# A two-layer DiT block on one Trainium2 core: a new order for the mixer's second half, half a product moved ahead of a norm in the latents, and other PSUM banks behind the attention

## The chip, the cores and the metric

The kernel runs on one core of one Trainium2 chip. The core has five engines that each work through an instruction queue of their own: TensorE (PE in the profile, matrix products; PEld is the loading of its stationary operand), VectorE (DVE), ScalarE (ACT), GpSimd (POOL) and SyncE (SP, which issues the DMA transfers here). They meet through semaphores. Products land in PSUM, eight banks of 128 partitions x 512 fp32 numbers; all other data of the core lie in SBUF.

The metric is the device time of one launch in microseconds (us); lower is better. The kernel before takes 1628.01 us, the median of three runs from 1627.53 to 1628.06.

## The reference, cut to what matters

Batch 1, 512 tokens of width 1024, a context of 256 tokens, fp32 throughout. Layer 0 mixes tokens with a Fourier half and a Hyena half, on tokens and context; layer 1 is multi-head latent attention (16 heads) from the tokens to tokens and context. Each layer ends in a feed-forward network with a convolution of three taps.

```python
for i in range(2):
    sh1, sc1, g1, sh2, sc2, g2 = split(silu(c) @ w_mod[i] + b_mod[i], 6)      # and the same for the context
    hx = rms_norm(x, norm1[i]) * (1 + sc1) + sh1
    if i == 0:
        proj = hx @ w_in                                    # 1024 -> 2048
        y_f = fft2(proj[:, :512] by groups of 128, axes=(tokens, features)).real
        x0, x1, v = split(dwconv3(proj[:, 512:]), 3)        # three times 512
        y_h = x0 * long_conv(v * x1, spectrum, hy_bias)     # irfft(rfft(u) * spectrum)
        yx = concat(y_f, y_h) @ w_out
    else:
        a = hx @ mla_w_in                                   # 256 query latents, 128 + 32 of keys and values
        yx = softmax(q k^T / sqrt(96)) v @ mla_w_o          # q, k, v from the latents, each rms-normed
    x = x + g1 * yx
    x = x + g2 * ((silu(dwconv3(gate)) * val) @ w_down)     # gate, val = split(modulated rms_norm(x) @ w_up, 2)
```

The Fourier transforms are products with tables of cosines and sines on TensorE, folded by symmetry, so that the mixer is a chain of products with elementwise work between them.

## The kernel before, in words

**Products.** Every matrix is kept as a high and a low part (`wh`, `wl` of a weight `wr`; `hh`, `hl` of an activation), and `mm3` adds three products: high by high (line 158), high weight by low activation (159), low weight by high activation (160). ScalarE writes the high part (`hi`, line 133), VectorE the low one (`lo`, line 138; in the mixer some lows go to GpSimd). Weights come in by `wraw` (line 146) from SyncE's queue into three buffers `wr`, and are split into three buffers each of `wh` and `wl`. TensorE gets 128 partitions a time.

**PSUM.** A pool holds tiles by tag: `mm` has three buffers of two banks, `ms` two buffers of one bank. Which banks a tag has follows from the order in which the tags are first used after a pool was opened. In the attention another pool (`psB`) is open; it is closed in `layer1`, where `psA` is opened again.

**Mixer's second half** (about 219 to 313 us of the span). The order of work on TensorE, VectorE, ScalarE and GpSimd is written out: `MIX_ORDER` is a list of short step names, each of which records its instructions when its turn comes; nothing reorders them afterwards. The DMA steps (R) stand in the same list. The names:

- `P6q`, `P7q`: projection of row block 6 or 7, two of the eight steps over the width (six products each, 512 and 260 columns wide) per name, into an `mm` tile. `CAm`, `CBm`, `CCm`: the convolution of block m, on ScalarE (line 863), then twice on VectorE (865, 867).
- `FM`: x1 times v on GpSimd (871, 872). `FD`: its sums and differences on VectorE (878, 879). `T3`: six transposes on TensorE (887). `UH`, `UL`: high and low part of the result, `uTh`, `uTl`.
- `SC0`, `SC1`, `SX0` to `SX3`: spectra of context (C) and tokens (X), products of `uTh`, `uTl` with the table `u`, into `mm`. For each: `DA`, `DB` on VectorE (918, 919, 921), which multiply by the filter's spectrum into `sx`; `QA`, `QB` on GpSimd (926); `YA`, `YB` the high part on ScalarE; `LA` the low part on VectorE, `LB` on GpSimd.
- `IC0` to `IC3`, `IX0` to `IX3`: inverse transforms into `ms`. Each is followed by `..E` on ScalarE, `..S` on VectorE (961, 962), `..M` on VectorE (967), `..H` on ScalarE and `..L` on VectorE, which give `yh` and `yl` of row blocks 4 to 7.
- `FHg`, `FLg`: high and low part of the Fourier half's group g. `FAg`, `GAg`: its first transform, tokens and context, into `mm`; `PH`, `PL` and `GH`, `GL` (1014) the high and low parts `pqh`, `pql`. `FBg`, `GBg`: the second transform; `FE`, `GE` on ScalarE, `FS`, `GS` on VectorE (1040 to 1042).
- `WH`, `WL`, `TH`, `TL`: high and low parts of weights and tables. `ZHg`, `ZLg`: those of row blocks 0 to 3. `OA`, `OB0` to `OB3`: the first column block of the output product, over row blocks 4 to 7, then 0 to 3.

While this runs, VectorE also has a few row sums of the modulation (`gemv_dve`, line 243), recorded between these steps.

**Latents** (in `attention`, lines 1343 to 1375). `qa(k)` adds step k of the query latents, for two row blocks m (three products of 512 columns each), into one `mm` tile. `take(KD)` and `f2(tp, 0)` end the sums of squares of the second half's norm: each has TensorE multiply the last squares by ones (line 280, `ms<-ones,nt`), after which VectorE finishes the sum (283, 285) and does a reciprocal root of twelve small instructions (167 to 176); `f2(tp, 1)` spreads the result with TensorE (298). The order is again the written one.

**Behind the attention** (`layer1`). The last output product leaves row blocks 0 and 1 in a PSUM tile `k` (`pre` in the code) of `psB`. The residual `xr` is loaded back (line 1723), VectorE adds the two row blocks to it (1725), then `psA` is opened and `res_proj` does row blocks 2 to 7 in two halves of 256 tokens (eight steps, 24 products per block and half; line 1143 takes the tile away), while the norm of the first half runs in its hook. Then the feed-forward network follows.

Of the kernel before, what the change touches and what calls it, by code (L numbers as in the profile page):

```python
# [72 lines left out]
KAx3 G3 KBx3 SDAx2 RG4 SQx2 G4 SDAx0 SPBx2 KAx2 SPBx0 SDBx2 SQx0 KBx2 SDBx0  # L73
"""
MIX_ORDER = """
P11 R6 R7 WH6 WL6 P60 CA11 P61 CB11 CC11 P62 FM Ru0 WH7 FD T3 P63 WHu0 UH CA6 WL7 UL WLu0 CB6 SC0 Ru1 CC6 DBc0 SC1 DAc1 QBc0 YBc0 LBc0 WHu1 Ri0 Rn1
P70 QAc1 YAc1 WLu1 P71 DAc0 P72 QAc0 P73 YAc0 WHi0 SX0 LAc1 DBc1 HP QBc1 Rs0 LAc0 WLi0 SX1 CA7 YBc1 THn1 LBc1 CB7 DBx0 IC0 QBx0 DAx0 TLn1 IC1 QAx0 FH0
Rc0 THc0 ICE0 THs0 YBx0 ICE1 YAx0 Rn0 CC7 ICS0 LBx0 IC2 FL0 ICS1 TLs0 Rc1 IC3 THn0 LAx0 GA0 DAx1 DBx1 QAx1 SX2 GH0 QBx1 FA0 GL0 TLc0 THc1 YAx1 YBx1
LBx1 LAx1 FH1 TLn0 TLc1 DAx2 DBx2 SX3 PH0 GB0 ICM0 FH2 QAx2 QBx2 PL0 YAx2 ICH0 YBx2 LAx2 FL1 DAx3 GE0 ICE2 LBx2 DBx3 ICL0 FL2 FB0 FA1 FE0 GS0 PH1 QAx3
Ri1 GA1 QBx3 FS0 ICM1 PL1 YBx3 ICH1 FA2 WHi1 ICL1 ICE3 FB1 ICS2 LBx3 WLi1 GH1 YAx3 PH2 GL1 GA2 LAx3 Ro0 FE1 IX1 PL2 GB1 ICS3 ICM2 IXE1 IX0 IXS1 FH3  # L80
FS1 ICH2 ICM3 GH2 ICH3 ICL2 IXM1 IXH1 IXE0 ICL3 IX2 GE1 IXS0 FB2 FL3 GS1 IXE2 IXM0 GL2 FA3 FE2 IXH0 IXS2 IX3 IXM2 IXH2 FS2 GA3 PH3 IXL1 IXL0 PL3 IXL2
IXE3 IXS3 GB2 WHo0 IXM3 IXH3 FB3 GH3 GE2 FE3 WLo0 GL3 GB3 GE3 ZH0 IXL3 GS2 FS3 GS3 OA ZL0 OB0 ZH1 ZL1 ZH2 ZH3 OB1 ZL2 ZL3 OB2 OB3
"""


class Builder:
# [1182 lines left out]
    def attention(self, x, hh, hl, steps, aw):  # L1269
# [72 lines left out]
        with self.tc.manual_schedule(engines={ENG.PE, ENG.DVE, ENG.Activation, ENG.Pool}):  # L1342

            pqa = self.mm()

            def qa(k):
                for m in range(2):
                    wh, wl = aw[f"qa{m}"]
                    w = slice(128 * k, 128 * k + 128)
                    self.mm3(pqa[:, 512 * m : 512 * m + 512], wh[:, w], wl[:, w], hh[k][:, 0:T], hl[k][:, 0:T], k == 0, k == KD - 1)  # L1350

            def down(ps, h, l, m, k, c0, n):
                w = slice(m * k, m * k + m)
                self.mm3(ps[:m, c0 : c0 + n], h[:, w], l[:, w], hh[k][:, c0 : c0 + n], hl[k][:, c0 : c0 + n], k == 0, k == KD - 1)

            qa(0)
            qa(1)
            qa(2)
            take(KD)
            qa(3)  # L1360
            f2(tp, 0)
            wph, wpl = self.t(pt, [P, 512], F32R, "whpe", 1), self.t(pt, [P, 512], F32R, "wlpe", 1)
            self.hi(wph, wp[:, :512])
# [350 lines left out]
    def layer1(self, x, hh, hl, steps, aw):  # L1714
        nc, I = self.nc, self.I
        oh, ol, xd, pre = self.attention(x, hh, hl, steps, aw)
        nt = self.pool("nt", bufs=5)
        hp = self.pool("h2p")
        self.xp = self.pool("xres")
        tp = lambda: self.t(nt, [P, 512], F32, "nt")  # L1720
        x = [self.t(self.xp, [P, T], F32, f"xr{d}") for d in range(KD)]
        for d in range(KD):
            nc.sync.dma_start(x[d], xd[d])
        for m in range(2):
            nc.vector.scalar_tensor_tensor(x[m], pre[:, 512 * m : 512 * m + 512], self.mod[1][:, 16 + m, 0:1], x[m], op0=ALU.mult, op1=ALU.add)
        self.close("psB")
        self.ps = self.pool("psA", space=PSUM)
        half = [[(0, 256)], [(256, 256)]]
        hh = [self.t(hp, [P, T], F32R, f"hh{d}") for d in range(KD)]
        hl = [self.t(hp, [P, T], F32R, f"hl{d}") for d in range(KD)]  # L1730
        hook, rest = self.norm_hook(*[self.norm(1, 1, x, hh, hl, c, 256, tp) for c in (0, 256)])
        self.res_proj(1, 2, oh, ol, KD, lambda m: I["w_o"][m], x, half, hook, ready=2)
        rest()
        self.close("pO")
        self.close("pa")
        self.dbg("xa1", x)
        self.ffn(1, x, hh, hl, T, [(0, T)], half, None)
        return x
# [204 lines left out]
```

## Time and profile before

| | |
|---|---|
| median of three runs | 1628.01 us (1627.53 to 1628.06) |
| the profiled execution | 1633.3 us, its span 1631.5 us |
| mean granted TensorE clock | 0.991 |
| TensorE busy | 1589.6 us, 97% of the span |
| VectorE busy | 1048.2 us, 64% |
| ScalarE busy | 620.1 us, 38% |
| GpSimd busy | 109.5 us, 7% |
| mixer's second half | about 219 to 313 us |
| latents' query products and second norm | about 942 to 963 us |
| residual product behind the attention | about 1213 to 1257 us |

A line of the timeline has the start in us, the duration, the engine, the line of the code, the operation with output and inputs, the sizes, and in brackets how long the engine stood idle before it and what ended the wait. Durations overlap a little with the next row's start, since matmuls and VectorE's instructions are pipelined; the rate is read from start to start. A group over a stretch (`--windows` answers) has the busy time of each engine, the number of its instructions, the granted clock of TensorE (1.00 is full speed, 0.50 half) and the share of DMA.

### The profile page before, as it was taken

What the parts mean: (1) busy time and instruction counts of PE and PEld (TensorE: products, weight loads), DVE (VectorE), ACT (ScalarE), POOL (GpSimd) and SP (SyncE); (2) the same over time, 40 slices, a digit from 0 to 9 for tenths busy, and PEclk for the clock granted to TensorE, in tenths of its full rate; (3) what the DMA queues carried; (4) which work ended last, traced back from release to release, by engine and by line L of the source; (5) the groups of instructions that cost most, each with busy time, mean ns of one, the idle gap of its engine ahead of it and who ended that gap; (6) DMA issues with size and microseconds to landing.
All of it is one profiled execution on the core that took longest, in us unless ns stands there. A gap on an engine that the chain in (4) does not pass through costs nothing.

```text
span 1631.5 us, 20800 instructions
## 1 busy us (share of the span) xinstructions
PE 1589.6 (97%) x8248; PEld 1300.2 (80%) x8248; DVE 1048.2 (64%) x1702; ACT 620.1 (38%) x883; POOL 109.5 (7%) x165
## 2 busy tenths in 40 slices
PE   7999998999999999999999999999989999999999
PEld 5687888888888888888888887566559888888887
DVE  5788869878786354643354577899977544344243
ACT  4451224424222212222133337898953432233131
POOL 0112134000000000000000001121210000000000
PEclk9999998999999999999999999999999999999999
DMA  9336412533443243432342210000033232222222
GB/s 344 108 117 211 170 36 72 194 117 106 166 155 129 66 141 129 159 125 71 108 147 99 95 55 16 13 11 13 0 129 116 78 103 102 80 104 98 83 91 90
DMA packets 54542, 173.35 MB, mean 106 GB/s; under 512 B 6188, under 2 KB 9454, under 8 KB 53422
## 3 DMA queue, kind: packets, MB, share of 16 engines
q1 hardware_dynamic: 54445, 172.03, 30.5%
q8 instruction: 65, 1.06, 0.3%
q14 instruction: 32, 0.25, 0.0%
HBM read 166.24 MB, written 5.77 MB: 105 GB/s over the span
## 4 chain that ended last, share of the span: by engine, by line
PE 81%; DVE 13%; DMA 2%; issue 2%; ACT 1%; POOL 1%; SPq 0%; POOLq 0%; ACTq 0%; DVEq 0%
PE mm L158 24%; PE mm L159 23%; PE mm L160 23%; PE pv L1613 2%; DVE junk L243 2%; DVE S L1589 1%; DVE wl L138 1%; PE s L1559 1%; DVE wr L1628 1%; DMA wr<-w_in 1%; PE k L158 1%; PE k L159 1%; PE k L160 1%; DMA wm<-wmod0a 1%; PE mm L616 1%
## 5 line engine op out<-in xcount | busy, mean ns | idle before, releaser
L158 PE MATMUL mm<-hh,wh 128*128 128x512 f32 (+2 forms) x1360 | 480.9, 356 | 1.8 <-ACT wh L133 0.9
L159 PE MATMUL mm<-hl,wh 128*128 128x512 f32 (+2 forms) x1360 | 478.6, 353 | 2.3 <-DVE hl L313 2.3
L160 PE MATMUL mm<-hh,wl 128*128 128x512 f32 (+2 forms) x1360 | 478.4, 352 | 1.6 <-DVE wl L138 1.6
L133 ACT ACTIVATE wh<-wr 128x1024 fp32r<-128x1024 f32 (+1 forms) x192 | 197.8, 1033 | 579.8 <-PE mm L159 544.6
L138 DVE TENSOR_TENSOR wl<-wr,wh 128x1024 fp32r<-128x1024 f32 (+2 forms) x192 | 231.2, 1207 | 234.9 <-ACT wh L133 228.3
L158 PEld LDWEIGHTS mm<-hh,wh 128*128 128x128 f32 x1360 | 256.6, 189 | 48.4 <-issue 7.6
L159 PEld LDWEIGHTS mm<-hl,wh 128*128 128x128 f32 x1360 | 257.1, 189 | 39.2 <-DVE hl L313 3.5
L160 PEld LDWEIGHTS mm<-hh,wl 128*128 128x128 f32 x1360 | 256.9, 189 | 37.5 <-DVE wl L138 2.2
L243 DVE SCALAR_TENSOR_TENSOR junk<-wr,sb 128x1024 bf16<-128x1024 f32 x128 | 156.2, 1220 | 41.2 <-DMA wr<-wmodT 40.7
L158 PE MATMUL mm<-ah,wh 128*128 128x512 f32 (+1 forms) x480 | 172.4, 359 | 0.0
L160 PE MATMUL mm<-ah,wl 128*128 128x512 f32 (+1 forms) x480 | 172.2, 359 | 0.0
L159 PE MATMUL mm<-al,wh 128*128 128x512 f32 (+1 forms) x480 | 171.9, 359 | 0.0
L1143 DVE SCALAR_TENSOR_TENSOR xr<-mm,mod,xr 128x512 f32<-128x512 f32 (+1 forms) x100 | 61.8, 632 | 160.6 <-PE mm L160 160.1
L159 PEld LDWEIGHTS mm<-al,wh 128*128 128x128 f32 x480 | 90.5, 189 | 14.2 <-DVE al L138 0.2
L158 PEld LDWEIGHTS mm<-ah,wh 128*128 128x128 f32 x480 | 90.4, 188 | 14.1 <-issue 0.3
L160 PEld LDWEIGHTS mm<-ah,wl 128*128 128x128 f32 x480 | 90.4, 188 | 14.2
L1613 PE MATMUL pv<-S,V 128*128 128x512 f32 x192 | 93.9, 598 | 2.5 <-ACT S L1592 2.5
L1175 ACT ACTIVATE fg<-fg 128x772 f32<-128x772 f32 (+1 forms) x44 | 32.6, 741 | 98.0 <-DVE fg L375 91.4
L1567 ACT ACTIVATE S<-s,rks 128x512 f32<-128x512 f32 x96 | 62.6, 685 | 12.4 <-PE pv L1613 8.5
L1613 PEld LDWEIGHTS pv<-S,V 128*128 128x128 f32 x192 | 34.5, 190 | 34.7 <-issue 29.3
L1589 DVE TENSOR_TENSOR S<-S,mx 128x1536 f32<-128x1536 f32 x32 | 55.4, 1750 | 2.3 <-POOL mx L1585 2.3
L1585 POOL PARTITION_ALL_REDUCE mx<-mx x16 | 44.9, 2806 | 161.6 <-DVE mx L1582 161.6
(337 smaller groups left out, 2273.2 us busy)
## 6 DMA issues: line engine op xcount, KB each, us to landing
wr<-w_up SPq DMA_DIRECT2D x88, 512.0 KB, 3.2
wr<-wmodT SPq DMA_DIRECT2D x80, 512.0 KB, 3.2
wr<-w_dn SPq DMA_DIRECT2D x32, 512.0 KB, 3.2
wm<-wmod0a SPq DMA_DIRECT2D x8, 1024.0 KB, 8.9
wr<-w_in SPq DMA_DIRECT2D x16, 512.0 KB, 4.2
wr<-w_out SPq DMA_DIRECT2D x13, 512.0 KB, 3.7
wr<-w_dn SPq DMA_DIRECT2D x17, 384.0 KB, 3.0
wr<-w_o SPq DMA_DIRECT2D x11, 512.0 KB, 3.2
```

Source lines behind the costliest of these rows:

```text
L133: self.nc.scalar.activation(dst, src, AF.Copy)
L138: (eng or self.nc.vector).tensor_tensor(dst, src, hi.bitcast(F32), op=ALU.subtract)
L158: mmul(out, wh, xh, start=start, stop=False)
L159: mmul(out, wh, xl, start=False, stop=False)
L160: mmul(out, wl, xh, start=False, stop=stop)
L243: nc.vector.scalar_tensor_tensor(junk, raw, 1.0, self.sb[:, j, :], op0=ALU.mult, op1=ALU.mult, accum_out=acc)
L1143: nc.vector.scalar_tensor_tensor(x[m][:, a2:b2], ps[:, a2:b2], mod[:, 8 * sec + m, c : c + 1], x[m][:, a2:b2], op0=ALU.mult, op1=ALU.add)
L1175: nc.scalar.activation(g[:, :n], g[:, :n], AF.Silu)
L1567: nc.scalar.activation(c.S[a][j // 3][:, j % 3, :], c.ps[a, j], AF.Copy, scale=c.r[:, g : g + 1])
L1585: nc.gpsimd.partition_all_reduce(c.m[a][:, 1, :], c.m[a][:, 0, :], P, bass.bass_isa.ReduceOp.max)
L1589: v.tensor_tensor(c.S[a][h], c.S[a][h], mb.to_broadcast([P, 3, T]), op=ALU.subtract)
L1613: nc.tensor.matmul(c.P[a], V[:, j, o : o + 128], c.S[a][j // 3][:, j % 3, :], start=j == 0, stop=j == 5)
```

## The change

It has three parts. No instruction of the computation is added or removed; the sizes are the same.

**1. `MIX_ORDER` is written anew.** The same steps stand in another order, on all engines. The first two lines of the list, of before and after:

```diff
 MIX_ORDER = """
-P11 R6 R7 WH6 WL6 P60 CA11 P61 CB11 CC11 P62 FM Ru0 WH7 FD T3 P63 WHu0 UH CA6 WL7 UL WLu0 CB6 SC0 Ru1 CC6 DBc0 SC1 DAc1 QBc0 YBc0 LBc0 WHu1 Ri0 Rn1
-P70 QAc1 YAc1 WLu1 P71 DAc0 P72 QAc0 P73 YAc0 WHi0 SX0 LAc1 DBc1 HP QBc1 Rs0 LAc0 WLi0 SX1 CA7 YBc1 THn1 LBc1 CB7 DBx0 IC0 QBx0 DAx0 TLn1 IC1 QAx0 FH0
...
+P11 R6 WH6 R7 WL6 CA11 CB11 CC11 P60 FM P61 Ru0 FD T3 P62 WH7 UH P63 WHu0 CA6 Ru1 UL WL7 WLu0 CB6 SC0 CC6 DAc0 SC1 P70 P71 QAc0 YAc0 DAc1 LAc0 P72
+DBc0 QAc1 QBc0 Ri0 YAc1 LAc1 WHu1 DBc1 WLu1 Rs0 P73 YBc0 WHi0 CA7 QBc1 SX0 HP WLi0 Rn0 YBc1 CB7 THn0 SX1 LBc0 LBc1 Rn1 DBx0 DAx0 IC0 THs0 THn1 QBx0
...
```

TensorE had the products of block 6 with `T3` between P62 and P63; in the new list `T3` stands between P61 and P62. After this come SC0, SC1, P70 to P73, SX0, SX1, IC0, IC1 in both, then before "IC2 IC3 GA0 SX2 FA0 SX3 GB0 FB0 FA1 GA1 FA2 FB1 GA2 IX1 GB1 IX0 IX2 FB2 FA3 IX3 GA3 GB2 FB3 GB3" and now "IC2 FA0 IC3 SX2 GA0 SX3 FB0 FA1 GB0 GA1 FB1 FA2 GB1 IX2 GA2 FB2 IX0 FA3 GA3 IX3 GB2 IX1 FB3 GB3", and OA, OB0 to OB3 in both.

Three places. TensorE's queue around `T3`, about 223 us of the span. `hh4`, `hh5`, `hh6` are the steps over the width (two steps make one name), line 887 is `T3`. Before:

```order
L159 MATMUL mm_408_1978<-hl5_111_370,wh_406_1974 128x260
L160 MATMUL mm_408_1978<-hh5_110_369,wl_407_1975 128x260
L887 MATMUL mm_414_2031<-cst_2_69,tm_413_2026 128x128 x6
L158 MATMUL mm_408_1978<-hh6_112_371,wh_406_1974 128x512
L159 MATMUL mm_408_1978<-hl6_113_372,wh_406_1974 128x512
```

The transposes stand behind step 5, which ends P62. Now:

```order
L159 MATMUL mm_408_1981<-hl3_107_366,wh_405_1972 128x260
L160 MATMUL mm_408_1981<-hh3_106_365,wl_406_1973 128x260
L887 MATMUL mm_412_2016<-cst_2_69,tm_411_2011 128x128 x6
L158 MATMUL mm_408_1981<-hh4_108_367,wh_405_1972 128x512
L159 MATMUL mm_408_1981<-hl4_109_368,wh_405_1972 128x512
```

The twelve products of steps 4 and 5 have moved from ahead of the transposes to behind them.

VectorE's queue at the mixer's end, the last instructions ahead of `ZL0` (`yl0`). `pql4` is GL3, `yl5` and `yl7` are IX1's and IX3's low parts, `wl_615`, `wl_625` are weights of the product that follows, lines 1040 to 1042 are GS and FS, line 243 is a row sum of the modulation. Before:

```order
L138 TENSOR_TENSOR wl_567_2846<-wr_538_2606,wh_566_2845 128x1024
L138 TENSOR_TENSOR wl_615_3069<-wr_613_3066,wh_614_3068 128x1024
L138 TENSOR_TENSOR wl_625_3113<-wr_623_3110,wh_624_3112 128x1024
L1014 SCALAR_TENSOR_TENSOR pql4_570_2876<-mm_560_2813,pqh4_569_2875 128x512
L138 TENSOR_TENSOR yl7_449_2198<-s2_564_2829,yh7_448_2197 128x512
```

Between these and `yl0` there stood only nine instructions of FS and GS and the two row sums. Now:

```order
L961 TENSOR_TENSOR s2_571_2879<-e_569_2846,ms_568_2820 128x256
L962 TENSOR_TENSOR s2_571_2879<-e_569_2846,ms_568_2820 128x256
L138 TENSOR_TENSOR wl_615_3069<-wr_613_3066,wh_614_3068 128x1024
L967 TENSOR_TENSOR s2_571_2879<-s2_571_2879,x1_17_110 128x512
L138 TENSOR_TENSOR yl7_449_2200<-s2_567_2816,yh7_448_2199 128x512
L138 TENSOR_TENSOR wl_625_3113<-wr_623_3110,wh_624_3112 128x1024
L138 TENSOR_TENSOR yl5_445_2196<-s2_571_2879,yh5_444_2195 128x512
```

IX1's steps (the first two rows, line 967 and `yl5`) have become the last of the inverse transforms, with the two weights among them; `pql4` and the row sums now stand ahead of this piece, and six instructions of FS and GS behind it, then `yl0`.

**2. `qa(3)` is split.** Its first row block now stands ahead of the first fold of the norm.

```diff
-            def qa(k):
-                for m in range(2):
+            def qa(k, ms=(0, 1)):
+                for m in ms:
                     wh, wl = aw[f"qa{m}"]
                     w = slice(128 * k, 128 * k + 128)
                     self.mm3(pqa[:, 512 * m : 512 * m + 512], wh[:, w], wl[:, w], hh[k][:, 0:T], hl[k][:, 0:T], k == 0, k == KD - 1)
@@ ...
             qa(2)
+            qa(3, (0,))
             take(KD)
-            qa(3)
+            qa(3, (1,))
             f2(tp, 0)
```

TensorE's queue there, about 947 us of the span; line 280 is the fold, `hh3`, `hl3` belong to step 3. Before:

```order
L160 MATMUL mm_1391_8326<-hh2_594_3009,wl_1362_8212 128x512
L280 MATMUL ms_1393_8347<-ones32_3_71,nt_1349_8161 128x1 x2
L158 MATMUL mm_1391_8326<-hh3_595_3010,wh_1354_8174 128x512
L159 MATMUL mm_1391_8326<-hl3_603_3018,wh_1354_8174 128x512
L160 MATMUL mm_1391_8326<-hh3_595_3010,wl_1355_8175 128x512
L158 MATMUL mm_1391_8326<-hh3_595_3010,wh_1361_8211 128x512
```

Now:

```order
L160 MATMUL mm_1391_8326<-hh2_594_3009,wl_1362_8212 128x512
L158 MATMUL mm_1391_8326<-hh3_595_3010,wh_1354_8174 128x512
L159 MATMUL mm_1391_8326<-hl3_603_3018,wh_1354_8174 128x512
L160 MATMUL mm_1391_8326<-hh3_595_3010,wl_1355_8175 128x512
L280 MATMUL ms_1393_8350<-ones32_3_71,nt_1349_8161 128x1 x2
L158 MATMUL mm_1391_8326<-hh3_595_3010,wh_1361_8211 128x512
```

Three products have changed places with the fold; all else in the queue is as it was.

**3. An `ms` tile is taken first behind the attention.**

```diff
         self.close("psB")
         self.ps = self.pool("psA", space=PSUM)
+
+        self.ms()
         half = [[(0, 256)], [(256, 256)]]
```

The tile is never written or read. Since `ms` is now the first tag of the pool, it has banks 0 and 1, and the three `mm` buffers have banks 2 to 7 in place of 0 to 5: the first `mm` tile (row block 2) lies in banks 2 and 3, where it lay in 0 and 1, the banks of `pre`. No engine's queue changes.

More of the change, by code (lines that the diff above doesn't have):

```diff
@@ L75 @@
 MIX_ORDER = """
-P11 R6 R7 WH6 WL6 P60 CA11 P61 CB11 CC11 P62 FM Ru0 WH7 FD T3 P63 WHu0 UH CA6 WL7 UL WLu0 CB6 SC0 Ru1 CC6 DBc0 SC1 DAc1 QBc0 YBc0 LBc0 WHu1 Ri0 Rn1
-P70 QAc1 YAc1 WLu1 P71 DAc0 P72 QAc0 P73 YAc0 WHi0 SX0 LAc1 DBc1 HP QBc1 Rs0 LAc0 WLi0 SX1 CA7 YBc1 THn1 LBc1 CB7 DBx0 IC0 QBx0 DAx0 TLn1 IC1 QAx0 FH0
[L78 to L82, printed above, removed]
+P11 R6 WH6 R7 WL6 CA11 CB11 CC11 P60 FM P61 Ru0 FD T3 P62 WH7 UH P63 WHu0 CA6 Ru1 UL WL7 WLu0 CB6 SC0 CC6 DAc0 SC1 P70 P71 QAc0 YAc0 DAc1 LAc0 P72
+DBc0 QAc1 QBc0 Ri0 YAc1 LAc1 WHu1 DBc1 WLu1 Rs0 P73 YBc0 WHi0 CA7 QBc1 SX0 HP WLi0 Rn0 YBc1 CB7 THn0 SX1 LBc0 LBc1 Rn1 DBx0 DAx0 IC0 THs0 THn1 QBx0
+FH0 ICE0 CC7 ICS0 YBx0 TLs0 FL0 IC1 ICE1 QAx0 ICS1 Rc0 YAx0 IC2 LBx0 LAx0 DAx1 FA0 TLn0 IC3 QAx1 THc0 PH0 DBx1 YAx1 ICM0 Rc1 ICH0 SX2 ICM1 TLn1 QBx1
+GA0 LAx1 YBx1 PL0 DAx2 LBx1 Ro0 DBx2 GH0 QAx2 QBx2 FH1 THc1 YAx2 TLc0 SX3 TLc1 FL1 LAx2 GL0 FB0 ICH1 YBx2 LBx2 FE0 DAx3 QAx3 DBx3 FA1 FH2 FS0 GB0 ICL0
+PH1 YAx3 GE0 QBx3 PL1 Ri1 GA1 ICE2 ICL1 YBx3 LBx3 FL2 ICE3 GH1 GS0 ICS2 WHi1 FB1 FA2 LAx3 GL1 WLi1 FE1 FS1 GB1 PH2 ICM2 IX2 ICH2 GA2 ICS3 ICM3 PL2 FB2
+ICL2 GE1 GH2 FH3 FE2 ICH3 IXE2 GS1 FL3 IX0 GL2 FA3 ICL3 IXS2 IXE0 FS2 IXS0 PH3 IXM2 GA3 IX3 WHo0 IXM0 IXH0 GB2 IXH2 PL3 WLo0 IXE3 GH3 GE2 IXS3 IXL2
+IX1 IXM3 IXE1 IXH3 IXL0 GL3 GS2 FB3 IXS1 IXM1 IXH1 GB3 FE3 IXL3 IXL1 GE3 FS3 GS3 ZH0 ZH1 ZH2 OA ZL0 ZL1 ZL2 OB0 ZH3 ZL3 OB1 OB2 OB3
 """
```

## The prediction

> **What bounds the kernel now.** I read the page's head first, then TensorE's waits, then the stretches that the change touches.
>
> ```profile
> span 1631.5 us, 20800 instructions
> PE 1589.6 (97%) x8248; PEld 1300.2 (80%) x8248; DVE 1048.2 (64%) x1702; ACT 620.1 (38%) x883; POOL 109.5 (7%) x165
> PE 81%; DVE 13%; DMA 2%; issue 2%; ACT 1%; POOL 1%; SPq 0%; POOLq 0%; ACTq 0%; DVEq 0%
> ```
>
> TensorE is busy for 97% of the span and carries 81% of the chain that ended last. It can gain 42 us of idle time at most, and what it loses to a lower clock, which counts as busy. So each part is priced by TensorE's waits and clock in its own stretch. The stretches (mixer's second half in four, latents, three behind the attention):
>
> ```profile
> core 0: us, PE busy (x) PEld busy (x) DVE busy (x) ACT busy (x) POOL busy (x), PEclk, DMA share, GB/s
> 219.00:238.00 19.00, 18.57 (x104) 15.74 (x103) 13.48 (x18) 6.28 (x7) 5.61 (x5) 1.00 0.13 42
> 238.00:259.00 21.00, 18.34 (x96) 16.66 (x95) 18.34 (x28) 9.05 (x16) 12.87 (x25) 0.79 0.15 45
> 259.00:281.00 22.00, 19.03 (x129) 17.31 (x128) 21.59 (x34) 10.43 (x20) 10.02 (x7) 0.97 0.23 79
> 281.00:313.00 32.00, 29.80 (x228) 28.11 (x228) 31.68 (x71) 15.38 (x28) 1.83 (x48) 1.00 0.37 126
> 940.00:960.00 20.00, 18.64 (x91) 15.55 (x90) 15.32 (x40) 7.64 (x16) 0.19 (x4) 0.91 0.34 102
> 1213.00:1223.00 10.00, 6.55 (x31) 6.08 (x30) 4.41 (x6) 3.19 (x5) 0.00 (x0) 0.66 0.87 333
> 1223.00:1233.00 10.00, 10.00 (x86) 10.00 (x85) 6.74 (x11) 3.99 (x7) 0.00 (x0) 1.00 0.43 142
> 1233.00:1243.00 10.00, 10.00 (x87) 10.00 (x86) 4.59 (x14) 1.90 (x3) 0.00 (x0) 1.00 0.05 18
> ```
>
> From 238 to 313 us VectorE is busy for 18.34 + 21.59 + 31.68 = 71.6 of 75 us: in this stage it is VectorE, not TensorE, that sets the end. The clock is below 1 in just three of these stretches, and in each of them TensorE had waited.
>
> **Part 3, the banks.** The timeline there, TensorE and two of VectorE's rows:
>
> ```profile
> 1213.32 0.40 PE L160 MATMUL k<-Oh,wl 128*128 128x512 f32 x1
> 1217.17 0.58 PE L158 MATMUL mm<-Oh,wh 128*128 128x256 f32 x1 [3.44 <-DVE xr L1725]
> 1217.55 0.42 PE L159 MATMUL mm<-Ol,wh 128*128 128x256 f32 x1
> 1217.76 0.41 PE L160 MATMUL mm<-Oh,wl 128*128 128x256 f32 x1
> 1228.61 0.48 DVE L1143 SCALAR_TENSOR_TENSOR xr<-mm,mod,xr 128x256 f32<-128x256 f32 x1 [0.26 <-PE mm L160]
> 1231.46 0.48 DVE L1143 SCALAR_TENSOR_TENSOR xr<-mm,mod,xr 128x256 f32<-128x256 f32 x1 [0.27 <-PE mm L160]
> ```
>
> TensorE waits 3.44 us until line 1725 has read `k`, whose banks the first `mm` tile takes. Then it runs at half clock: starts 0.21 us apart, where a block of 24 products at full clock takes 2.85 us (1228.61 to 1231.46), 0.12 each. A clock of 0.66 over the 10 us to 1223 is 6.8 us at half; of these it works in the 5.8 from 1217.2 to 1223.0, so 2.9 us are lost. With the tile in other banks it goes on at 1213.55, and row blocks 2, 3, 4 would end at 1216.4, 1219.25 and 1222.1. What is late next is block 5's weight:
>
> ```profile
> 1215.31 15.90 SPq L146 DMA_DIRECT2D wr<-w_o  x5
> wr<-w_o SPq DMA_DIRECT2D x1, 512.0 KB, 6.3
> 1222.48 1.06 ACT L133 ACTIVATE wh<-wr 128x1024 fp32r<-128x1024 f32 x1 [4.92 <-PE mm L159]
> 1223.57 1.23 DVE L138 TENSOR_TENSOR wl<-wr,wh 128x1024 fp32r<-128x1024 f32 x1 [0.39 <-ACT wh L133]
> ```
>
> SyncE issues it at 1215.31, behind the eight residual loads, and it lands 6.3 us later, at 1221.6 (no queue moves, so this stays). Its high part is then ready at 1222.7 and its low part at 1223.9, while TensorE needs the low part at 1222.3: a new wait of 1.6 us. Blocks 6 and 7 follow in time. Gain: 3.44 + 2.9 - 1.6 = **4.7 us**. If the half clock isn't met in the timed runs, it is 3.44 - 1.6 = 1.8. VectorE has 3.3 and 5.4 us free in the two stretches behind and its work there hangs on TensorE's tiles, so it moves along and nothing is given back.
>
> **Part 2, the latents.**
>
> ```profile
> 948.25 0.61 PE L280 MATMUL ms<-ones,nt 128*128 128x1 f32 x4 [1.36 <-DVE nt L274]
> 952.11 0.63 PE L160 MATMUL mm<-hh,wl 128*128 128x512 f32 x1
> 952.54 0.63 PE L158 MATMUL mm<-hh,wh 128*128 128x512 f32 x1
> 954.79 0.40 PE L160 MATMUL mm<-hh,wl 128*128 128x512 f32 x1
> 955.02 0.61 PE L298 MATMUL ms<-cst,rq_r 128*128 128x128 f32 x4
> 951.29 0.16 DVE L283 SCALAR_TENSOR_TENSOR nrm_s<-ms,nrm_s 128x2 f32<-128x2 f32 x1 [1.57 <-PE ms L280]
> 953.46 0.16 DVE L176 SCALAR_TENSOR_TENSOR rq_r<-rq_b,rq_r 128x2 f32<-128x2 f32 x1
> ```
>
> The fold waits 1.36 us for VectorE; three products (0.23 us from start to start, as 954.79 to 955.02; 0.69 in all) move into this wait. Behind it stands a stretch at half clock (starts 0.43 apart at 952.1; the stretch's mean clock of 0.91 over 20 us means 0.09 x 20 x 2 = 3.6 us at half, so 1.8 lost; one such window costs 1.7). With half the idle time gone I take the window as gone too: 0.69 + 1.7 = **2.4 us**, or 0.7 if it isn't. The root that line 298 needs (2.3 us from 951.29) then starts about 1 us earlier and ends at 952.6, when TensorE gets there: the cover just holds.
>
> **Part 1, the order.** Its first effect is a loss:
>
> ```profile
> 223.39 0.39 PE L158 MATMUL mm<-hh,wh 128*128 128x512 f32 x1
> 225.49 0.82 PE L887 MATMUL mm<-cst,tm 128*128 128x128 f32 x6
> 225.47 0.28 DVE L879 TENSOR_TENSOR tm<-tm 128x128 f32<-128x128 f32 x1
> 236.58 1.48 DVE L138 TENSOR_TENSOR wl<-wr,wh 128x1024 fp32r<-128x1024 f32 x1 [1.89 <-ACT wh L133]
> 239.91 1.27 DVE L138 TENSOR_TENSOR s<-sx,s 128x512 fp32r<-128x512 f32 x1 [0.66 <-ACT s L133]
> ```
>
> The twelve products from 223.39 to 225.49 now stand behind `T3`, which TensorE reaches at 223.4, but its input still ends with line 879 at 225.7: TensorE stands for about 2.0 us. VectorE's own idle time before 240 us (1.89 + 0.66 = 2.5) takes this up, so that VectorE comes into its full stretch when it did before. From there the end is set by VectorE's sum:
>
> ```profile
> 242.90 2.32 DVE L138 TENSOR_TENSOR wl<-wr,wh 128x1024 fp32r<-128x1024 f32 x1
> 251.42 0.45 PE L158 MATMUL ms<-wh,s 128*128 128x128 f32 x1 [2.66 <-DVE e L962]
> 258.83 0.69 DVE L1014 SCALAR_TENSOR_TENSOR pql<-mm,pqh 128x512 fp32r<-128x512 f32 x1 [1.97 <-ACT pqh L135]
> 309.00 3.57 DVE L138 TENSOR_TENSOR yl<-x,yh 128x772 fp32r<-128x772 f32 x4
> 310.01 0.50 PE L159 MATMUL mm<-yl,wh 128*128 128x512 f32 x1 [0.90 <-DVE yl L138]
> ```
>
> The longest wait of TensorE, 2.66 us for IC0's sums, shrinks to under 1, since ICS0 stands earlier and IC2 comes later; with it goes some of the half clock (0.79 over the stretch). But TensorE then meets VectorE's next deadlines. VectorE has the same instructions to do before `yl0`. What it can save is its one long wait, 1.97 us for GH0: GL0 now stands behind TLc0, TLc1, FL1 and LAx2, and FA0, whose PL0 comes ahead of it, ahead of IC3. So `yl0` comes at 307.0 instead of 309.0, and the product of 310.01 at about 308: **2.0 us**. At the end IX1 is the last inverse transform, and OA's second step waits for `yl5`; that is queued about 1.3 us ahead of `yl0`, and OA's three steps left take 3 x 0.69 us, so this wait is inside the other. Bounds: a gain of 3.4 (all of VectorE's idle time, 75 - 71.6) plus what less GpSimd beside it saves; a `wl` beside GpSimd took 2.32 us, the one of 1223.57 took 1.23, so about half of GpSimd's time can come on top. GpSimd's 12.87 + 10.02 + 1.83 = 24.7 us would cost 12.4 if all of it met such work; no view sums what is already paid (the 2.32 alone shows 1.1), and I take half, 6.2. That gives -9.6 to +6.2, and a clock window behind `T3` adds 1.7, of which 0.5 is covered: up to +7.4.
>
> **Sum.** -4.7 - 2.4 - 2.0 = -9.1 us against the profiled execution's 1633.3, so 1624.2 there. The median is 5.3 us below that execution; carried over, 1628.0 - 9.1 = **1618.9 us**.
>
> A rule that bears on it: the Trainium skill's "TensorE: Matmul & The Clock Gate" (section "HAM oscillation — how this bites in real kernels") warns of TensorE gaps over about 3.4 us. The gap of 3.44 agrees; those of 2.66 and 1.36 were shorter and half clock followed too, so the trace is stricter here. By the page the latents' window isn't the gap's doing: part 2 would bring 0.7 and the time would be 1620.6.
>
> **Rivals.** (a) The half clock isn't a matter of these waits, or is rarer in timed runs, which are 5.3 us faster than the profiled one: parts 3 and 2 bring idle time alone, 1.8 + 0.7, and with the mixer's 2.0 the time is 1623.5. The differing sizes of the waits ahead of half clock speak for it; that it follows a wait in all three stretches speaks against. The page's rule is half of this.
>
> (b) The mixer gives more: GpSimd meets less of VectorE's work, -6 instead of -2: 1614.9. For it: the stretched rows are there to be saved. Against: GpSimd has the same work in the same stretch.
>
> (c) Other side: VectorE's stretch grows, as QA, QB and LB meet its low parts and inverse sums more often. Every us lands on `yl0`. It decides where the mixer loses over 10.4 us with the other parts as forecast (1631.3 = 1628.0 - 7.1 + 10.4), or over 5.8 with parts 2 and 3 at their low ends; at +7.4 and those it gives 1632.9, at +4 with half of the window gains about 1627. For it: VectorE has no slack from 240 us on, and TensorE's list has three new deadlines (`T3`, SX3 behind PL0, OA behind `yl5`). Against: the same instructions, 24.7 us of GpSimd in both.
>
> (d) The bank change doesn't act, should the second wait be as long as the first (the weight later than 1221.6): part 3 brings 1, the time is 1622.6.
>
> **Chances.** Forecast 0.42 (1616 to 1622); (a) 0.18; (d) 0.07; (b) 0.08; (c) 0.25, half of it slower than before. A measurement of this kernel tells 0.2%, 3.3 us, from no change: faster than 1624.8, slower than 1631.3. (a) crosses 1624.8 in a sixth of its cases, (c) lies a tenth on the fast side. Faster 0.74, same 0.13, slower 0.13. The range from 1613 to 1630 leaves 0.2 out, half on each side.
>
> **What would show it.** Part 3: no wait on line 1725, a wait of about 1.6 us for a `wl` near 1222 less what came before, clock 1.00 in that stretch. Part 2: the fold's wait near 0.7, line 298 2.4 us earlier against `qa(0)`. Part 1: a wait of 2 us at line 887; no 2.66 before IC2; `yl0` 2 us earlier from P11. Wrong it goes if half clock follows `T3` or OA, if VectorE's rows from 240 to 305 us are longer in sum, or if block 5's weight lands later.

## The result, and the profile after

The changed kernel takes 1631.71 us (median of 8 runs, 1630.34 to 1636.04); the kernel before took 1628.07 us beside it (8 runs, 1627.53 to 1629.34). The ratio is 1.0022, 95% interval 1.0012 to 1.0033: 3.6 us slower. The forecast was 9 us faster.

The two profiled executions are 1633.3 us (before) and 1632.75 us (after), so they alone would hide the loss: that of before lies 5.3 us above the median of its three runs, and has half clock in the latents that two other traces of the same code lack (below). What follows is therefore read from intervals inside a trace, and the prices come from timed kernels. The page's head and the stretches of the changed kernel, the latter with the same columns as before and one stretch more (960 to 1000, the attention's start):

```profile
span 1631.0 us, 20799 instructions
PE 1586.7 (97%) x8248; PEld 1296.2 (79%) x8248; DVE 1049.4 (64%) x1702; ACT 620.9 (38%) x883; POOL 110.6 (7%) x165
PE 79%; DVE 16%; issue 2%; ACT 1%; DMA 1%; POOL 1%; SPq 0%; POOLq 0%; DVEq 0%; ACTq 0%
```

```profile
219.00:238.00 19.00, 16.89 (x93) 14.17 (x93) 14.05 (x20) 5.22 (x7) 4.74 (x5) 1.00 0.10 35
238.00:259.00 21.00, 19.89 (x114) 17.61 (x113) 20.37 (x28) 10.42 (x17) 15.29 (x26) 0.92 0.19 55
259.00:281.00 22.00, 17.79 (x128) 16.20 (x128) 22.00 (x37) 10.65 (x20) 8.90 (x6) 1.00 0.23 81
281.00:313.00 32.00, 28.26 (x198) 25.94 (x198) 30.30 (x65) 13.64 (x24) 1.84 (x48) 0.89 0.40 135
940.00:960.00 20.00, 19.34 (x115) 16.80 (x114) 17.59 (x44) 8.84 (x19) 0.19 (x4) 1.00 0.35 103
960.00:1000.00 40.00, 37.18 (x213) 30.72 (x211) 25.66 (x63) 15.06 (x27) 3.65 (x7) 0.91 0.06 21
1213.00:1223.00 10.00, 9.45 (x48) 7.42 (x47) 7.31 (x7) 3.98 (x6) 0.00 (x0) 1.00 0.51 181
```

Two stretches got better, as forecast: the latents (clock 0.91 before, 1.00 now) and the place behind the attention (TensorE 6.55 of 10 us busy at 0.66 before, 9.45 at 1.00 now; the same 10 us hold earlier work now, but the first product on `mm`, at 1221.22, follows without a wait and at full clock). Two got worse: the mixer's end (281 to 313: TensorE 29.80 busy at full clock before, 28.26 at 0.89 now), and the attention's start, of which the prediction does not speak. There the kernel before had

```profile
960.00:1000.00 40.00, 39.34 (x254) 32.83 (x253) 27.86 (x73) 18.98 (x38) 3.65 (x7) 1.00 0.07 21
```

The waits and rows that make the difference, first in the mixer (timeline of the changed kernel: `T3`, then OA's second step and VectorE's first `yl0`):

```profile
222.94 0.98 PE L887 MATMUL mm<-cst,tm 128*128 128x128 f32 x6 [1.58 <-DVE tm L878]
305.97 0.80 PE L158 MATMUL mm<-yh,wh 128*128 128x512 f32 x1 [2.79 <-ACT yh L133]
307.64 0.79 PE L159 MATMUL mm<-yl,wh 128*128 128x512 f32 x1 [0.88 <-DVE yl L138]
308.66 0.63 PE L158 MATMUL mm<-yh,wh 128*128 128x512 f32 x1
309.09 0.63 PE L159 MATMUL mm<-yl,wh 128*128 128x512 f32 x1
311.22 1.05 PE L158 MATMUL mm<-yh,wh 128*128 128x512 f32 x2
308.69 0.95 DVE L138 TENSOR_TENSOR yl<-x,yh 128x772 fp32r<-128x772 f32 x1
```

TensorE stands 1.58 us at `T3`. At the end it stands 2.79 us for IX1's high part (`yh5`) and 0.88 for its low part; then the products run 0.43 us apart, at half clock, until 311.2, although `yl0` was there at 309.6.

The wait at IC2, 2.66 us in the kernel before, is down to

```profile
PE ms L158 <- DVE e L962: 0.7, 1, 0.7
```

Then the attention's first product:

```profile
983.40 1.00 DVE L1437 SCALAR_TENSOR_TENSOR kp<-mm,pcol,ropeK 64x772 f32<-64x772 f32 x1
984.46 0.36 PE L158 MATMUL k<-wh,qah 128*128 128x192 f32 x1 [2.66 <-DVE kp L1437]
984.65 0.27 PE L159 MATMUL k<-wl,qah 128*128 128x192 f32 x1
985.34 0.42 PE L158 MATMUL k<-wh,qah 128*128 128x192 f32 x1
985.56 0.42 PE L159 MATMUL k<-wl,qah 128*128 128x192 f32 x1
```

It waits 2.66 us for line 1437 (1436 in the kernel before), VectorE's read of the positional key product, and goes over to half clock (0.22 us apart) behind it. The kernel before had no wait here. The reason is in no engine's queue: it is in the banks, as the built programs give them. In both kernels `k` lies in banks 0 and 1. In the kernel before, the three last `mm` tiles ahead of it (query latents, key and value latents, positional key) lay in banks 0, 4 and 2; in the changed kernel they lie in 2, 4 and 0. The new order of the mixer has two of the three `mm` buffers change places, and all that comes behind inherits it. Before, `k` took the banks of the query latents, last read some eight us before (until 972.4, `k` starts at 980.4); now those of the positional key, read last.

### The profile page after: what moved, and what is told of

The parts are those of the page before. It is cut to its first block, busy times and chain, and to the rows that moved or that the text cites. A ratio compares the mean times of both kernels' runs of the same rounds, so it can differ in the third digit from the quotient of the medians.

```text
span 1631.0 us, 20799 instructions
## 1 busy us (share of the span) xinstructions
PE 1586.7 (97%) x8248; PEld 1296.2 (79%) x8248; DVE 1049.4 (64%) x1702; ACT 620.9 (38%) x883; POOL 110.6 (7%) x165
## 4 chain that ended last, share of the span: by engine, by line
PE 79%; DVE 16%; issue 2%; ACT 1%; DMA 1%; POOL 1%; SPq 0%; POOLq 0%; DVEq 0%; ACTq 0%
PE mm L158 23%; PE mm L159 23%; PE mm L160 23%; DVE junk L243 2%; PE pv L1614 2%; DVE wl L138 2%; DVE S L1590 2%; PE s L1560 1%; DVE wr L1629 1%; DVE hl L313 1%; DMA wm<-wmod0a 1%; PE k L159 1%; PE mm L616 1%; PE k L158 1%; PE k L160 0%
```

## The experiments

Every ratio is to runs of the kernel before made beside it, and differences are given in us of 1629.

### Each part apart

`e1_order` has the kernel before with the new `MIX_ORDER` alone.

> The kernel before with the new MIX_ORDER alone. Theory W (what the two traces show is what the timed runs have): the mixer ends about 4 us later against its start, since OA's second step waits 2.8 us for yh5 and 0.9 for yl5 and a window at half clock follows; and the new order swaps two of the three mm buffers for all that comes behind, so that the first tile of the attention (k) takes the banks of the positional key product and waits 2.7 us for line 1436 with 3 us of half clock behind it. Together +10 us, about 1638. Theory I (in timed runs waits cost their idle time alone, half clock is rarer): about +2 in the mixer and +2.7 in the attention, about 1633. If the swap of the banks isn't a result of the order, the wait at k is absent here and the time is about 1632 under W.

It took 1644.31 us, ratio 1.0080 (1.0065 to 1.0095): 13.0 us slower, more than either theory. The wait at `k` is there (2.68 us, line 1436), so the swap of the banks comes from the order. Behind it the clock was 0.81 over the 40 us, where the changed kernel had 0.91; why it stayed at half so much longer is not shown:

```profile
940.00:960.00 20.00, 18.64 (x113) 16.27 (x112) 16.89 (x41) 8.55 (x18) 0.19 (x4) 1.00 0.35 101
960.00:1000.00 40.00, 37.32 (x197) 31.30 (x196) 22.93 (x60) 15.49 (x28) 3.65 (x7) 0.81 0.08 22
```

`e3_ms` has part 3 alone, `e4_split_ms` parts 2 and 3; both keep the old order.

```diff
 self.ps = self.pool("psA", space=PSUM)     # e3_ms, e4_split_ms, in layer1
+self.ms()
...
-            take(KD)                       # e4_split_ms only, with qa(k, ms=(0, 1))
-            qa(3)
+            qa(3, (0,))
+            take(KD)
+            qa(3, (1,))
```

> The kernel before with the first ms tile behind the attention alone (part 3). Theory W: the wait of 3.44 us for line 1725 and the half clock behind it go, and about 1.6 us of them come back as a wait for block 5's weight: 1628 - 4.7 = 1623.4; without the new wait 1622. Theory I: 3.4 less the new wait, 1625 to 1626.

1623.70 us, ratio 0.9956 (0.9942 to 0.9970): 7.2 us faster (4.9 to 9.4). TensorE's rows there, and ScalarE's on the weights that follow (the last two rows: `wh` of row blocks 5 and 6):

```profile
1211.01 0.40 PE L160 MATMUL k<-Oh,wl 128*128 128x512 f32 x1
1211.24 0.28 PE L158 MATMUL mm<-Oh,wh 128*128 128x256 f32 x1
1211.36 0.28 PE L159 MATMUL mm<-Ol,wh 128*128 128x256 f32 x1
1215.42 1.05 ACT L133 ACTIVATE wh<-wr 128x1024 fp32r<-128x1024 f32 x1
1219.58 1.06 ACT L133 ACTIVATE wh<-wr 128x1024 fp32r<-128x1024 f32 x1 [2.21 <-DMA wr<-w_o]
```

TensorE goes from `k` to `mm` without a wait and at full clock, and the forecast wait of 1.6 us does not come. Block 5's high part starts at 1215.42, as soon as its buffer is free: its weight had been issued ahead of the residual loads. The weight that lands late is block 6's (ScalarE waits 2.21 us for it), and that one has time.

> The kernel before with parts 2 and 3, without the new order. Theory W: part 2 adds 2.2 us of gain (the two traces: 3.4 us behind at the fold, 1.2 behind at the spread) to that of part 3: 1620 to 1621. Theory I: 0.7 more than part 3 alone, 1624 to 1625.

1621.39 us, ratio 0.9949 (0.9935 to 0.9963), 1.1 us less than part 3 alone, within the intervals. The traces settle it better. From the first product of `qa(0)` to the third of the spread's four (line 298) pass 12.68 us in the kernel before, 11.11 in `e1_order` and in `e3_ms`, neither of which has the split, 10.40 in `e4_split_ms` and in the changed kernel. The split brings 0.71 us. The other 1.57 are the window at half clock of the kernel before, which `e1_order` (its first row above) and `e3_ms` don't have, with the same wait of 1.4 us at the fold:

```profile
PE ms L280 <- DVE nt L274: 1.4, 1, 1.4
940.00:960.00 20.00, 18.63 (x96) 15.37 (x94) 16.32 (x44) 8.43 (x18) 0.19 (x4) 1.00 0.32 102
```

So the old order with parts 2 and 3 is 8.3 us faster than the kernel before, and 11.9 faster than the changed one: all of the loss, and more, is the order's.

### The banks

`e5_pv_first` keeps all three parts and moves only the attention's banks: a `pv` tile is taken first in its pool, so that `k` gets banks 2 and 3, those of the query latents in the new order. Behind the attention the first `mm` tile then has banks 0 and 1, free of `k`, without the extra `ms` tile.

```diff
+            PV()
             q0 = K2()
...
-        self.ms()
```

> All three parts, but the banks of the attention shifted: a pv tile is taken first in its pool, so that k lies in banks 2 and 3 (those of the query latents, read early) and not in 0 and 1; part 3's tile behind the attention is then not needed and is left out, since the first mm tile has banks 0 and 1, free of k. Theory W: the wait at k and its half clock go, 5 to 6 us less than the changed kernel, about 1626. Theory I: 2.7 us less, about 1629. If the wait at k hangs on line 1436 by something else than banks, no difference.

1628.71 us, ratio 0.9993 (0.9984 to 1.0002): 4.7 us less than the changed kernel. The wait at `k` is gone, and half of the half clock with it (0.96 over the 40 us for 0.91):

```profile
PE ms L280 <- DVE nt L274: 0.7, 1, 0.7
PE pv L158 <- ACT V L1606: 0.5, 1, 0.5
960.00:1000.00 40.00, 39.51 (x234) 32.20 (x233) 29.74 (x78) 17.41 (x32) 3.65 (x7) 0.96 0.07 21
```

These two waits are all that TensorE has from 950 to 1010. The wait of 2.66 us and 0.05 of clock over 40 us, 2.0 us, make the 4.7. One stretch at half clock is left there without any wait at `k`; `e3_ms` and `e4_split_ms`, in the old order, have one too (0.94 from 975 to 1005). With the banks out of the way 7.2 us (4.5 to 9.9) are left between the new order and the old (`e4_split_ms`): the mixer's own loss.

### The mixer's loss

Counted in each trace from the first product of P60, in us: the start of the convolution's row CB7 on VectorE (both orders have about the same behind it), of `yl0` on VectorE, of the first product with `yl0`, and the end of the product of OB3.

| kernel | order | CB7 | `yl0` | product with `yl0` | end |
|---|---|---|---|---|---|
| before | old | 25.99 | 89.86 | 90.87 | 94.14 |
| e4_split_ms | old | 26.00 | 89.49 | 90.50 | 93.80 |
| after | new | 26.44 | 91.73 | 95.12 | 98.58 |
| e5_pv_first | new | 26.45 | 92.83 | 95.78 | 98.98 |
| e6_swap13 | new, IX1 and IX3 exchanged | 26.46 | 91.65 | 92.66 | 95.93 |
| e7_t3_back | new, `T3` back | 25.38 | 90.62 | 94.02 | 97.48 |
| e10_swap_t3 | new, both | 25.37 | 90.76 | 91.97 | 95.16 |
| e9_old_noq | old, no QA, QB | 23.50 | 82.98 | 83.99 | 87.28 |
| e8_new_noq | new, no QA, QB | 25.88 | 84.99 | 88.38 | 91.63 |

In the old order TensorE's product follows `yl0` by 1.0 us; in the new it comes 3.0 to 3.4 us behind. So 2 to 2.4 us are lost on TensorE, and 2 to 3 on VectorE, where `yl0` itself is later. The changed kernel and `e5_pv_first` have the same order here and still differ by 1.1 us in `yl0`; the latter has more half clock ahead of it (0.74 against 0.91 from 245 to 265). Differences of that size between two traces prove nothing alone. `e6_swap13` takes up the first (all steps of IX1 and IX3 in each other's places), `e7_t3_back` puts `T3` behind P62 again; both on `e5_pv_first`.

```diff
-... IXE3 GH3 GE2 IXS3 IXL2
-IX1 IXM3 IXE1 IXH3 IXL0 GL3 GS2 FB3 IXS1 IXM1 IXH1 GB3 FE3 IXL3 IXL1 GE3 ...
+... IXE1 GH3 GE2 IXS1 IXL2
+IX3 IXM1 IXE3 IXH1 IXL0 GL3 GS2 FB3 IXS3 IXM3 IXH3 GB3 FE3 IXL1 IXL3 GE3 ...
```

> The kernel with the banks mended (pv first: 1628.7), with the inverse transforms IX1 and IX3 (all steps after the transform too) in each other's places, so that the low part that comes last is yl7, which OA needs for its last step, and not yl5, which it needs for its second. Theory T (tail): TensorE's 2.8 + 0.9 us of waiting at OA's second step and the nine products at half clock behind them set the mixer's end, 1.7 us behind yl0; with the late part needed two products of 0.7 us later, some 1.5 us go: 1627. Theory V (VectorE): yl0 itself is what the mixer ends on, so nothing changes: 1628.7.

1622.23 us, ratio 0.9964 (0.9952 to 0.9976): 4.7 us less, with an uncertainty of about 2.4. The tail is theory T's:

```profile
304.37 0.50 PE L159 MATMUL mm<-yl,wh 128*128 128x512 f32 x1 [2.45 <-DVE yl L138]
304.94 0.40 PE L158 MATMUL mm<-yh,wh 128*128 128x512 f32 x1
305.17 0.39 PE L159 MATMUL mm<-yl,wh 128*128 128x512 f32 x1
308.15 0.50 PE L159 MATMUL mm<-yl,wh 128*128 128x512 f32 x1 [0.82 <-DVE yl L138]
```

TensorE still waits 2.45 us in the same step, but earlier and at full clock behind it (0.23 us apart), so that it is at `yl0` in time. The product now follows `yl0` by 1.0 us, and the end lies 3.05 us earlier: 1.9 of it is the tail, near theory T's 1.5, and 1.2 an earlier `yl0`, which is as early as in the changed kernel and so not the exchange's. That the clock stayed full is not what mends the tail: in `e10_swap_t3` below a wait of 2.63 us in this place is followed by half clock, and the product still follows `yl0` by 1.2 us. The rest of the 4.7 is not in the mixer: the trace of `e5_pv_first` has one window each at half clock near 378 and 990 us, this one has not.

> The kernel with the banks mended, with T3 back behind P62. Theory V: VectorE's slack before 240 us had taken up TensorE's 1.6 us at T3, so the time stays at 1628.7 within 0.5. Theory P (TensorE's waits add up): 1.6 us faster, 1627.1.

1625.09 us, ratio 0.9978 (0.9969 to 0.9986): 2.4 us less, with an uncertainty of about 2. Theory V fails: VectorE's slack had not taken up the wait. CB7 comes 1.07 us earlier and `yl0` 2.2 (1.1 against the changed kernel). The path is VectorE's wait for ScalarE's step CA6, which follows P63 on TensorE. In the changed kernel and in the kernel before it is

```profile
DVE x L865 <- ACT x L863: 1.2, 1, 1.2
DVE x L865 <- ACT x L863: 0.2, 1, 0.2
```

and with `T3` back there is none. TensorE then waits as long elsewhere (SC0 for `wl`, 1.57 us; 0.4 in the old order), yet VectorE is ahead.

> The kernel with the banks mended, with both mends of the new order: IX1 and IX3 exchanged (alone 1622.2, against 1628.7) and T3 back behind P62 (alone 1625.1). By the traces, counted from P60, the product's last column ends at 98.98 us with the banks mended, 95.93 with the exchange, 97.48 with T3 back, and 93.80 in the old order. Theory A (two separate losses, the tail on TensorE and 1.1 to 2 us of VectorE's time that T3 costs): they add up: about 94.5 and 1620.5, even with parts 2 and 3 on the old order (1621.4) or better. Theory B (both mends remove the same half clock, not the same work): no better than the exchange alone, 1622.

1623.61 us, ratio 0.9955 (0.9943 to 0.9967): 6.2 us less than with the banks alone, where the two mends alone sum to 7.1. The step from the exchange alone is 1.5 us, inside the intervals, so timing does not tell theories A and B apart; in the trace `yl0` comes 0.9 us earlier than with the exchange alone. With both mends the mixer ends 1.4 us behind the old order (95.16 against 93.80), and the time is 1.0 us behind it, again within the intervals. By the times these two places so hold 6.2 of the 7.2 us, by the traces 3.8 of 5.2.

### GpSimd beside VectorE

The rest of VectorE's lateness can be GpSimd's. VectorE's subtractions for `wl`, `s` and the tables took up to 1.1 us longer than their shortest where GpSimd worked; summed over all rows from CC6 to `yl0`, by shape above the shortest of the shape, about 9.3 us in the new order and 7.4 in the old. The same operation in the changed kernel, twice:

```profile
251.48 0.68 DVE L138 TENSOR_TENSOR s<-sx,s 128x512 fp32r<-128x512 f32 x1
257.46 1.78 DVE L138 TENSOR_TENSOR s<-sx,s 128x512 fp32r<-128x512 f32 x1
```

The Trainium skill ("SBUF — State Buffer", section "SBUF: two separate sides") says that a VectorE instruction with two SBUF inputs and a GpSimd operation that reads SBUF shut each other out for a whole instruction. The trace agrees: beside the second row GpSimd does a subtraction of its own (LB, at 257.40, 1.30 us), near the 1.10 us more, while VectorE's products of 253.89 and 254.49, with one input in PSUM, take 0.68 us beside a sum on GpSimd. In `e8_new_noq` and `e9_old_noq` the twelve sums are left out:

```diff
         def QQ(c, s, ft):
+            return
```

> The kernel with the banks mended and the new order, with GpSimd's twelve sums QA and QB left out (the mixer's output is then not the reference's). To be compared with the next. VectorE's instructions that GpSimd stretches cost 9.3 us above their shortest durations in the new order and 7.4 in the old. Theory G (GpSimd beside VectorE is why the new order loses): without the sums both orders come close, within 2 us, and this one gains most: 1628.7 - 8 or so. Theory S (the order's own waits lose): the difference to the next stays near 7.

> Parts 2 and 3 with the old order (1621.4), with GpSimd's twelve sums QA and QB left out (the mixer's output is then not the reference's). Theory G: 4 to 6 us faster, and within 2 us of the one before. Theory S: as much faster as the one before, and still some 7 us ahead of it.

New order: 1620.98 us, ratio 0.9953 (0.9940 to 0.9966), 6.5 us less than with the sums. Old order: 1617.59 us, ratio 0.9930 (0.9918 to 0.9942), 3.1 less. The distance between the orders falls from 7.2 to 3.7 us, half-way between the two theories, with an uncertainty of about 4. In the traces `yl0` comes earlier by 7.8 us in the new order and 6.5 in the old, and TensorE's tail of 3.4 us stays in the new. So GpSimd is worth 6 to 8 us of VectorE's time in either order. Of what tells the orders apart it is by the traces a small part (`yl0` is still 2.0 us later in the new one), by the times it may be half. The sums took their waits with them (YA and YB on ScalarE wait for them), and the half clock from 245 to 265 is gone in both (0.74 with the sums, 1.00 without); neither is separated from the stretching here.

### Tries at a faster kernel

Three kernels on `e4_split_ms` move steps of the old order: GL0, for which VectorE waited 2.0 us, behind TLc0, LAx1, TLn0 and TLc1 (`e11_gl0_late`); then ICS0 and ICS1 ahead of TLn1, CC7 and FL0 as well (`e12_ics_early`); then all of `qa(3)` ahead of the fold (`e13_qa3_whole`).

> Parts 2 and 3 on the old order (1621.4), with one step moved: VectorE's GL0, for which it waited 2.0 us, now stands behind TLc0, LAx1, TLn0 and TLc1. Theory V (VectorE's sum sets the mixer's end): yl0 comes up to 2.0 us earlier and the time is 1619.5. Rival: what stands behind is late as well (GB0 waits for GL0, GpSimd meets other work), no change.

1623.35 us, ratio 0.9958 (0.9946 to 0.9970), no gain. The wait for `pqh` went, and those for `s` grew (the first row was 0.7 us, the third is new; the second was there before); VectorE's, from 225 to 310 us:

```profile
DVE s L138 <- ACT s L133: 2.6, 2, 2.0
DVE wl L138 <- ACT wh L133: 1.9, 1, 1.9
DVE s L961 <- ACT e L955: 0.9, 2, 0.7
```

`yl0` comes 90.96 us behind P60, where it came 89.49 before the step was moved.

> The one before with ICS0 and ICS1 also moved ahead of TLn1, CC7 and FL0 on VectorE, so that TensorE's wait of 2.7 us at IC2, which half clock followed in the traces of the old order, becomes less than 1. Theory V: the mixer's end is VectorE's, so this brings little over the one before (under 0.7). Theory P: the wait and its half clock were on the path, 2 to 4 us faster than the one before.

1622.31 us, ratio 0.9949 (0.9938 to 0.9961), 1.5 us less than the one before, within the intervals. TensorE's wait at IC2 fell from 2.6 to 1.0 us, the mixer's end came 0.9 us earlier: nearer to theory V than to P. It is no clean test: a wait of 3.3 us for line 919 stands beside it, 2.8 in the one before and 0.9 in `e4_split_ms`.

> The one before with the whole of qa(3) ahead of the first fold, both row blocks. The fold's wait was 0.67 us with one block moved, so the other three products (0.69 us) fill it: 0.7 us less than the one before; no change if the root behind the fold (2.3 us on VectorE) is then what TensorE waits for at the spread.

1624.02 us, ratio 0.9955 (0.9942 to 0.9967), no gain. From `qa(0)` to the spread it takes 10.08 us instead of 10.40: a third of a microsecond, which the timing can't tell.

The fastest are `e4_split_ms` and `e12_ics_early`, both at 0.9949: the kernel before with the split and the extra tile, 8.3 us faster than before. The new order is not part of it, and with it the gain is gone.

## Why the prediction was wrong, point by point

**Part 3 was right in kind and too small.** Forecast 4.7 us, measured 7.2 (4.9 to 9.4) alone; the trace shows the 3.44 us of idle time and 2.98 of half clock, 6.4 together (from the first product on `mm` to the third of the first half's spread 27.52 us before, 24.54 now). In `e1_order`, which still has this wait (3.18 us), the half clock costs 1.9. The term that failed is the new wait of 1.6 us: I took the first `w_o` issue behind the residual loads, at 1215.31, for block 5's weight. It is block 6's. Rival (d) falls with it.

**Part 2 was over-sized.** Its idle time was forecast as 0.69 us and is 0.71. The 1.7 us of half clock that I booked with it are not tied to the wait: of three traces with the same wait one has them and two have not. What put them there in the one is not shown. Rival (a) was right here. The rule of the Trainium skill ("TensorE: Matmul & The Clock Gate", section "HAM oscillation — how this bites in real kernels"), by which a wait of 1.36 us shouldn't cost the clock, agrees with the two; but half clock came behind the wait of 2.66 us at `k`, also shorter than its 3.4, in both kernels that have it.

**Part 1 had the wrong sign.** Forecast 2.0 us of gain; in the changed kernel it costs 11.9 (its time against `e4_split_ms`). The one forecast for TensorE that came true, IC2's wait (0.7 us for 2.7), did not move the end. Four steps failed:

- *What the order changes.* The prediction looked at the queues and nowhere asked which buffer a later tile gets. 4.7 us (`e5_pv_first`) came from a swap of two PSUM buffers 700 us downstream. It could have been seen: the bank of every tile can be read from the built program, which the prediction does for part 3 alone.
- *"This wait is inside the other."* OA's wait for `yl5` was held to be hidden ahead of `yl0`. The arithmetic took 0.69 us a step; after 3.7 us of standing, the steps ran at 1.28, half clock that the sum had not put there. The longer part of the standing, 2.79 us for `yh5`, was not in the sum either. The exchange of IX1 and IX3 brings 4.7 us, 1.9 of it in the tail.
- *`T3` taken up by VectorE's idle time.* Putting `T3` back brings 2.4 us; CB7 comes 1.1 us and `yl0` 0.9 to 2.2 us earlier. VectorE's idle time before 240 us was no slack: the chain from TensorE by ScalarE (P63, CA6) that feeds VectorE came later by the same stand, and VectorE's wait for it grew from 0.2 to 1.2 us. `T3`'s wait itself was 1.58 us for the forecast 2.0, and no half clock followed it.
- *VectorE's sum.* The wait of 1.97 us did go. In its place came 1.63 us for a row sum whose weight is issued 68.2 us behind P60, where it was 65.8, and about 2 us more of stretched instructions. `yl0` is 2 us later, not earlier.

```profile
DVE junk L243 <- DMA wr<-wmodT: 1.6, 1, 1.6
DVE sx L919 <- POOL sx L926: 0.6, 1, 0.6
```

These are all of VectorE's waits from 238 to 313 us in the changed kernel. Rival (c) had the sign, and named GpSimd and the new deadlines, `T3`, SX3, OA; of these `T3` and OA are shown, and GpSimd's part is small by the traces, open by the times. Its price for the mixer, up to +7.4, holds the 7.2 that were measured, but by luck: 6.2 of it was GpSimd's. What took the time out of the range is the swap of the banks, for which there was no rival.

A reading was wrong, too, without weight in the sum: four of the stretches shown have a clock below 1, not three. The 0.97 of 259 to 281 is the end of the half clock ahead of it.

What stays open: why some traces have windows at half clock near 378 and 990 us. It is not the order alone. From 370 to 385 the clock is 0.89 in `e3_ms` (old order) and `e5_pv_first` (new), and 1.00 in `e4_split_ms` (old) and `e6_swap13` (new); from 975 to 1005 it is 0.94 in `e3_ms` and `e5_pv_first`, and 1.00 in the kernel before and in `e6_swap13`.

## What to carry to other kernels

When steps are reordered, list not only the queues but the buffer that every later tile gets: here two of three buffers that changed places stayed so through the rest of the pool, and showed up 700 us later as a wait at the next one. Price a wait of TensorE by the clock behind it as well, but book a window at half clock as saved only if more than one trace has it. Where an engine is nearly gapless, its one long wait is not a gain in hand, since what follows has waits of its own.

## What the runs showed that I had not expected

Half clock depends on more than the length of the wait. Behind the same wait of 1.4 us at the fold one trace has a window (12.68 us to the spread), two have none (11.11). OA's wait of 2.79 and 0.88 us was followed by half clock, that of 2.45 us in `e6_swap13` was not, that of 2.63 us in `e10_swap_t3` was. In each trace the stretches at half clock last 3.41 us or a multiple of it, unless the trace ends first, and begin on one grid of that step (in the changed kernel at 189.74, 251.18, 305.80, 377.48, 985.05 and 991.88). The Trainium skill ("TensorE: Matmul & The Clock Gate", section "What's actually happening") says that the window that watches TensorE runs freely, so that its place against the kernel differs. The traces agree with that: counted from P60, the next step of the grid begins after 0.35 us in the kernel before, 2.42 in `e6_swap13` and 3.09 in `e5_pv_first`. How much idle time in a step brings half clock is not shown.

The mean clock alone does not give a run's time. Of the runs of the changed kernel, that of 1636.04 us had 0.989 and that of 1630.34 had 0.995, but that of 1630.71 had 0.991. A clock that is 0.004 lower over 1630 us is 6.5 us of clock, and the last two differ by 0.4 us. Either most of that half clock cost nothing where it fell, or something else made up for it; the timed runs do not show which.
